# First FFN's output product as seven products of half size, with the last three modulation rows moved, in a hybrid layer on one core

## The chip, the core and the metric

The kernel runs on one core of a Trainium2 chip. The metric is device time in microseconds (us) of one execution, as the median of several runs. PE is TensorE, DVE is VectorE, ACT is ScalarE, POOL is GpSimd, SP is SyncE (here it only issues DMAs). Every engine works through its own list of instructions in the order written at build time.

## What is computed

```python
sh1, sc1, g1, sh2, sc2, g2, sh3, sc3, g3 = split(silu(c) @ w_ada + b_ada, 9)   # nine rows of 1024
u = rms_norm(x, ffn1_norm_g) * (1 + sc1) + sh1
x = x + 0.5 * g1 * swiglu(u, ffn1_w_in, ffn1_w_out)          # first FFN, d_ff = 2816
u = rms_norm(x, mix_norm_g) * (1 + sc2) + sh2
z = u @ w_mix + b_mix                                        # conv, mLSTM and forgetting attention
...                                                          # give y_a and y_b
merged = sigmoid(g_a) * (y_a @ w_branch_a) + sigmoid(g_b) * (y_b @ w_branch_b)
x = x + g2 * (merged @ w_out)
u = rms_norm(x, ffn2_norm_g) * (1 + sc3) + sh3
x = x + 0.5 * g3 * swiglu(u, ffn2_w_in, ffn2_w_out)          # second FFN
```

x is 512 tokens by 1024, all float32; swiglu(u) is (silu(a) * b) @ w_out with a, b the halves of u @ w_in.

## The kernel before

**Products.** A float32 product is made of three matmuls (mm3, L106 to L110): each operand is split in a high part (wh, uh, hh: ACT, L89 for weights) and a low part (wl, ul, hl: DVE, L91 for weights), and high x high, high x low and low x high are summed in PSUM. A weight tile arrives in `raw` (three buffers, 512 KB each, issued by SP at L79), is split into `wh` and `wl` (four buffers each), and is then free.

**Stages on PE, in order.** start (the first three blocks of the first FFN, while x is normed); first FFN-in (65 to 276 us); first FFN's output product (276 to 403); the mixer's products, mLSTM and attention; the branches (862 to 950) and w_out (to 1003); second FFN-in (1010 to 1241); second FFN's output product (from 1241).

**FFN-in.** 22 blocks j of 128 hidden columns. Each has two gemms, for a and b, of 8 k x 3 = 24 matmuls of 128x512 (gemm_stat). In the first FFN, ffn_h turns both into `hh` and `hl` (128x512 for each block).

**First FFN's output product, token_gemm.** Two halves of 512 output columns; in each, 22 k x 4 token blocks x 3 matmuls of 128x512, 264, thus 528 in all. A token block's result is scaled by the gate and added to x (DVE, `rs` and `x`, L575 and L577), squared and summed (ACT, L209). In the last token block of the second half norm_half(0) is woven in: from `ss` the mean `v`, a root in ten small DVE operations, `xn` (L236), 16 transposes on PE (L260), and then `uh`, `uf`, `ul` (u_from, L245 to L247) for the first 256 tokens of the mixer's input.

**Second FFN's output product, pair_out.** It is made by Strassen's scheme in Winograd's form: the product's three dimensions are cut in halves, and seven products of half size stand for eight: 11 pairs of blocks x 7 products x 2 x 3 = 462 matmuls of 128x512. pair_h makes, for each pair of blocks, sums of the four quarters of h (tiles `E`, `A1`, `Ra`, `Rb`, later `A2` by pair_split), and pair_weights makes sums of the quarters of w_out beside FFN-in: 22 units u, each of two loads `s` of 256 KB, four DVE sums of 128x256 (L434 to L437) and one store of 512 KB to `ws` in DRAM (L439). Z, Y, X and W are the four quarters of the result: Z and Y the first 256 tokens, W and X the last.

**Modulation rows.** ada_row makes one row v of 1024 from eight raw tiles of w_ada: DVE multiplies each by its column of c and accumulates (`acc`, L282 and L284); at the end the 128 partitions are folded (`fo`, L290), split in `hl` (L292), summed by two matmuls with a column of ones (`oneR`, L296), added to the bias `br` (L297) and stored (L298). Rows 0 and 1 are made in start, 2 to 6 beside first FFN-in, 7 and 8 beside token_gemm. mod_cols reads two rows back for a norm.

**What sets the order.** The program is written block by block; `extra` and `mid` are called between gemms and advance the generators ada_row and pair_weights by a step. The framework then orders each engine's list by its own estimates of when inputs are ready, under `issue_after` constraints, so an engine's list differs from the order of the code; it is fixed at build time. A `raw` tile waits for the third-last one to be split.

Of the kernel before, what the change touches and what calls it, by code (L numbers as in the profile page):

```python
# [46 lines left out]
class Layer:  # L47
    def __init__(self, tc, es, A, out, dbg=None):
# [223 lines left out]
    def ada_row(self, v, pool, bank):  # L272

        nc, A = self.nc, self.A
        acc = pool.tile([P, D], F32, name=self.nm("acc"), tag="xn", bufs=2)
        br = pool.tile([1, D], F32, name=self.nm("br"), tag="xn", bufs=2)
        for k in range(NK):
            r = self.raw([P, D], [(lambda t: t, A["w_ada"][0, k * P:(k + 1) * P, v * D:(v + 1) * D])])
            if k == 0:
                nc.sync.dma_start(br, A["b_ada"][:, v * D:(v + 1) * D])  # L280
                with self.tc.issue_after(self.last_ul.ins):
                    nc.vector.tensor_scalar(acc, r, self.ccol[:, 0:1], None, op0=MUL)  # L282
            else:
                nc.vector.scalar_tensor_tensor(acc, r, self.ccol[:, k:k + 1], acc, op0=MUL, op1=ADD)  # L284
            if k == NK - 1:
# [3 lines left out]
                nc.scalar.activation(t[0:64, :], acc[64:P, :], AF.Copy)  # L289
                nc.vector.tensor_tensor(acc[0:64, :], acc[0:64, :], t[0:64, :], op=ADD)  # L290
                nc.scalar.activation(hl[0:64, :], acc[0:64, :], AF.Copy)
                nc.vector.tensor_tensor(hl[64:P, :], acc[0:64, :], hl[0:64, :], op=SUB)  # L292
# [8 lines left out]
    def mod_cols(self, v, gain):  # L301
# [4 lines left out]
        b = self.tbank()  # L306
# [14 lines left out]
    def ffn_h(self, ps_a, ps_b, j, c0, c1, hp, tp):  # L321
        nc = self.nc
        w = c1 - c0
        s = self.tmp(tp, "sl")
        nc.scalar.activation(s[:, :w], ps_a[:, c0:c1], AF.Silu)
        nc.vector.tensor_tensor(s[:, :w], ps_b[:, c0:c1], s[:, :w], op=MUL)
        nc.scalar.activation(self.hh[j][:, c0:c1], s[:, :w], AF.Copy)
        nc.vector.tensor_tensor(self.hl[j][:, c0:c1], s[:, :w], self.hh[j][:, c0:c1], op=SUB)
# [780 lines left out]
    def run(self):  # L1109
# [205 lines left out]
```

## Time and profile before

| | us |
|---|---|
| median of 3 runs | 1354.39 (1353.95 to 1356.48) |
| the profiled execution | 1354.64 |
| its span | 1352.9 |
| first FFN-in | 65 to 276 |
| first FFN's output product | 276.1 to 402.7 |
| second FFN-in | 1010 to 1241 |
| second FFN's output product, matmuls | 1241.0 to 1345.9 |

The time of an execution is 1.74 us longer than the span, which runs from the first to the last instruction of the profile. A line of the profile names a line of the code, the engine, the operation and the tile that is written, then the tiles that are read. A matmul's own duration (389 ns for 128x512) is longer than the step from one matmul to the next, since they are pipelined; the step is what a matmul costs.

### The profile page before, as it was taken

What the parts mean: (1) busy time and instruction counts of PE and PEld (TensorE: products, weight loads), DVE (VectorE), ACT (ScalarE), POOL (GpSimd) and SP (SyncE); (2) the same over time, 40 slices, a digit from 0 to 9 for tenths busy, and PEclk for the clock granted to TensorE, in tenths of its full rate; (3) what the DMA queues carried; (4) which work ended last, traced back from release to release, by engine and by line L of the source; (5) the groups of instructions that cost most, each with busy time, mean ns of one, the idle gap of its engine ahead of it and who ended that gap; (6) DMA issues with size and microseconds to landing.
All of it is one profiled execution on the core that took longest, in us unless ns stands there. A gap on an engine that the chain in (4) does not pass through costs nothing.

```text
span 1352.9 us, 17800 instructions
## 1 busy us (share of the span) xinstructions
PE 1328.6 (98%) x6520; PEld 1113.0 (82%) x6520; DVE 887.8 (66%) x1661; ACT 589.4 (44%) x978; POOL 46.0 (3%) x71
## 2 busy tenths in 40 slices
PE   7999999999999999999999999999999999999997
PEld 6788887887888888988888888888788888888886
DVE  6866666655558767987686876446475655545776
ACT  4532333322235755556565676333353222223642
POOL 2000000000011101000000000002010000000000
PEclk9999999999999999999999999999999999999999
DMA  9676556665634434444243442354436677763474
GB/s 290 187 225 187 179 178 212 218 201 183 200 86 105 129 91 126 116 131 121 74 140 86 113 141 78 110 183 159 140 110 183 212 232 219 228 189 139 171 247 166
DMA packets 245691, 219.30 MB, mean 162 GB/s; under 512 B 12706, under 2 KB 206914, under 8 KB 245604
## 3 DMA queue, kind: packets, MB, share of 16 engines
q1 hardware_dynamic: 245124, 218.09, 52.9%
q8 instruction: 51, 0.84, 0.2%
q14 instruction: 36, 0.29, 0.1%
q0 software_dynamic: 416, 0.06, 0.0%
q10 hardware_dynamic: 64, 0.02, 0.0%
HBM read 194.47 MB, written 23.66 MB: 161 GB/s over the span
## 4 chain that ended last, share of the span: by engine, by line
PE 86%; DVE 7%; ACT 3%; DMA 2%; issue 1%; SPq 0%; DVEq 0%; ACTq 0%
PE g L110 22%; PE g L108 22%; PE g L109 22%; PE t L110 4%; PE t L108 4%; PE t L109 4%; PE g L697 2%; PE t L1041 2%; PE t L1011 1%; DVE wl L91 1%; PE t L982 1%; PE t L983 1%; PE t L697 1%; DVE fq L961 1%; DMA h_d<-hn 1%
## 5 line engine op out<-in xcount | busy, mean ns | idle before, releaser
L89 ACT ACTIVATE wh<-raw 128x1024 fp32r<-128x1024 f32 x236 | 244.2, 1040 | 434.1 <-PE g L109 143.4
L91 DVE TENSOR_TENSOR wl<-raw,wh 128x1024 fp32r<-128x1024 f32 x236 | 290.0, 1231 | 188.2 <-ACT wh L89 168.6
L108 PE MATMUL g<-uh,wh 128*128 128x512 f32 (+2 forms) x984 | 370.6, 377 | 0.8 <-ACT wh L89 0.7
L110 PE MATMUL g<-uh,wl 128*128 128x512 f32 (+2 forms) x984 | 369.6, 376 | 1.0 <-DVE wl L91 1.0
L109 PE MATMUL g<-ul,wh 128*128 128x512 f32 (+2 forms) x984 | 369.6, 376 | 0.0
L110 PEld LDWEIGHTS g<-uh,wl 128*128 128x128 f32 (+1 forms) x984 | 184.7, 188 | 35.7 <-DVE wl L91 1.8
L108 PEld LDWEIGHTS g<-uh,wh 128*128 128x128 f32 (+1 forms) x984 | 184.8, 188 | 34.5 <-ACT wh L89 1.4
L109 PEld LDWEIGHTS g<-ul,wh 128*128 128x128 f32 (+1 forms) x984 | 184.9, 188 | 33.2
L108 PE MATMUL g<-wh,uh 128*128 128x512 f32 (+1 forms) x320 | 111.9, 350 | 0.0
L110 PE MATMUL g<-wh,ul 128*128 128x512 f32 (+1 forms) x320 | 111.1, 347 | 0.0
L109 PE MATMUL g<-wl,uh 128*128 128x512 f32 (+1 forms) x320 | 110.9, 347 | 0.0
L284 DVE SCALAR_TENSOR_TENSOR acc<-raw,ccol,acc 128x1024 f32<-128x1024 f32 x49 | 62.8, 1282 | 13.0 <-DMA raw<-in_w_ada_dram 12.1
L108 PEld LDWEIGHTS g<-wh,uh 128*128 128x128 f32 x320 | 60.5, 189 | 7.8 <-DVE tk L896 0.5
L110 PEld LDWEIGHTS g<-wh,ul 128*128 128x128 f32 x320 | 60.5, 189 | 7.7
L109 PEld LDWEIGHTS g<-wl,uh 128*128 128x128 f32 x320 | 60.5, 189 | 7.4
L108 PE MATMUL g<-yh,wh 128*128 128x512 f32 x128 | 50.4, 394 | 0.0
L110 PE MATMUL g<-yh,wl 128*128 128x512 f32 x128 | 50.2, 392 | 0.0
L109 PE MATMUL g<-yl,wh 128*128 128x512 f32 x128 | 49.7, 388 | 0.0
L993 ACT ACTIVATE S<-S,mn 128x128 f32<-128x128 f32 (+1 forms) x64 | 35.6, 557 | 18.5 <-DVE mn L985 9.5
L108 PE MATMUL g<-wh,hh 128*128 128x512 f32 x88 | 35.0, 398 | 0.0
L110 PE MATMUL g<-wh,hl 128*128 128x512 f32 x88 | 34.9, 396 | 0.0
L108 PE MATMUL t<-wh,hh 128*128 128x512 f32 x88 | 34.8, 396 | 0.0
(319 smaller groups left out, 2054.8 us busy)
## 6 DMA issues: line engine op xcount, KB each, us to landing
raw<-in_ffn_w_in_dram SPq DMA_DIRECT2D x82, 512.0 KB
raw<-in_w_ada_dram SPq DMA_DIRECT2D x56, 512.0 KB
raw<-in_w_mix_dram SPq DMA_DIRECT2D x48, 512.0 KB
raw<-in_ffn_w_out_dram SPq DMA_DIRECT2D x33, 512.0 KB
s<-in_ffn_w_out_dram SPq DMA_DIRECT2D x44, 256.0 KB
ws<-s SPq DMA_DIRECT2D x22, 512.0 KB
ar<-in_w_ada_dram SPq DMA_DIRECT2D x32, 256.0 KB
raw<-in_w_mix_dram SPq DMA_DIRECT2D x32, 256.0 KB
```

Source lines behind the costliest of these rows:

```text
L89: nc.scalar.activation(hi, src, AF.Copy)
L91: nc.vector.tensor_tensor(lo, src, hi, op=SUB)
L108: mm(ps, lh, rh, start=start, stop=False)
L109: mm(ps, lh, rl, start=False, stop=False)
L110: self.last_mm = mm(ps, ll, rh, start=False, stop=stop)
L284: nc.vector.scalar_tensor_tensor(acc, r, self.ccol[:, k:k + 1], acc, op0=MUL, op1=ADD)
L697: mm = nc.tensor.matmul(acc_ps[b], (wl if p == 1 else wh)[:, b % 2, s], self.ul[k] if p == 2 else self.uh[k], start=k == 0 and p == 0, sto ...
L961: nc.vector.scalar_tensor_tensor(lo, b[own, :], gc[own, :], d[own, :], op0=MUL, op1=SUB)
L982: nc.tensor.matmul(ps[:, :w], q[:, s], k[:, :w], start=True, stop=False)
L983: nc.tensor.matmul(ps[:, :w], q[:, s], kl[:, :w], start=False, stop=True)
L993: nc.scalar.activation(S[:, ws], S[:, ws], AF.Exp, scale=-1.0, bias=m, accum_out=sm[:, qb:qb + 1])
L1041: nc.tensor.matmul(po[:, q0:], vt[:, kb, i, :], Px[:, o:o + T - q0], start=n == 1, stop=n == 8)
```

## The change

The first FFN's output product is made by pair_out too. So ffn_h gives way to pair_h, and pair_weights for ffn1_w_out runs beside first FFN-in, a step at each `mid` and `extra`. To make room, rows 2 to 5 are made there (before: 2 to 6), rows 6 and 7 beside the branches (one step for each of 16 branch products, with `acc` in two halves of 512), and row 8 beside second FFN-in. pair_out gets `last`: after Y it calls norm_half(0), and X and W are finished behind it, with squares in place of stores. The bias row `br` now takes a buffer of the `raw` ring, `acc` has one buffer, both `s` tiles lie in places of later `A` tiles, and the sum of the two branches is taken by DVE where POOL did it.

```diff
-    def ada_row(self, v, pool, bank):
+    def ada_row(self, v, new, bank):
...
             if k == NK - 1:
+                br = self.wp.tile([1, D], F32, name=self.nm("br"), tag="raw", bufs=3)
                 nc.sync.dma_start(br, A["b_ada"][:, v * D:(v + 1) * D])
...
-            self.ffn_act(pa, pb, j, 0, T, hp, tp)
+            self.pair_h(pa, pb, j, 0, T, hp, tp)
...
-            t = ts[u] = hp.tile([P, 5, 256], F32, name=self.nm("s"), tag=f"A{NP - 1}", bufs=1) if u % 2 else                 tp.tile([P, 5, 256], F32, name=self.nm("s"), tag="st", bufs=1)
+            t = ts[u] = hp.tile([P, 5, 256], F32, name=self.nm("s"), tag=f"A{NP - 2 + u % 2}", bufs=1)
...
-        def store(tb, half):
+            return t
+        def store(tb, half, t):
+            if last:
+                self.x_sq(tb, half, t)
+                return
...
+            if n == "Y" and last:
+                last()
...
-        self.ntmp, self.xn_tiles, self.ffn_act, self.gb_tag = 5, self.xn_start, self.ffn_h, ("gb", 1)
+        self.ntmp, self.xn_tiles, self.gb_tag = 4, self.xn_start, ("gb", 2)
...
-                ada = (s for v in (2, 3, 4, 5, 6) for s in self.ada_row(v, tp, self.gbank))
+                ada = (s for v in (2, 3, 4, 5) for s in self.ada_row(v, lambda: self.acc_ffn(tp), self.gbank))
+                pw = self.pair_weights(A["ffn1_w_out"][0], hp)
                 def extra(j):
-                    next(ada, None)
-                    next(ada, None)
-                    if j % 8 == 7:
+                    for _ in range(1 if j % 5 == 3 else 2):
                         next(ada, None)
-                self.ffn_in(A["ffn1_w_in"][0], NJ0, hp, tp, extra)
+                    next(pw, None)
+                self.ffn_in(A["ffn1_w_in"][0], NJ0, hp, tp, extra, lambda: next(pw, None))
...
-                    ada = self.ada_row(7 + half, tp, bank)
-                    extra = lambda: next(ada, None)
-                    self.token_gemm(lhs, NJ, A["ffn1_w_out"][0], half, self.residual(0.5, 2, half, tp), 2 + half, extra,
-                                    (lambda: self.norm_half(0, tp, G2, sh2)) if half else None)
...
+                self.pair_out(A["ffn1_w_out"][0], 2, hp, tp, lambda: self.x_load(A["x"][0]),
+                              lambda: self.norm_half(0, tp, G2, sh2))
             self.norm_half(1, tp, G2, sh2)
...
+            ada = (s for v in (6, 7) for s in self.ada_row(v, lambda: [self.tmp(bp, "acc") for _ in range(2)], self.tbank))
             for m in range(NK):
+                next(ada)
                 ta.append(self.branch(m, 0, bp, yp.tile([P, T], F32, name=self.nm("ta"), tag="qk", bufs=16), sg[m] if m < 2 else None))
             for m in range(NK):
                 t = self.branch(m, 1, bp, None)
-                nc.gpsimd.tensor_tensor(t, t, ta[m], op=ADD)
+                next(ada)
+                nc.vector.tensor_tensor(t, t, ta[m], op=ADD)
...
+            ada = self.ada_row(8, lambda: self.acc_ffn(tp), self.tbank)
...
+            def extra(j):
+                if j % 2:
+                    next(ada, None)
+                next(pw, None)
```

**The order at three places.** Where a row is folded beside first FFN-in, before, this is the DVE's list (row 3; `hl_266` is the folded row, `sl_252<-g_245` the activation of a block, which reads the end of its gemm):

```order
L284 SCALAR_TENSOR_TENSOR acc_228_1156<-raw_264_1381,ccol_155,acc_228_1156 128x1024
L290 TENSOR_TENSOR acc_228_1156<-acc_228_1156,fo_265_1384 64x1024
L292 TENSOR_TENSOR hl_266_1385<-acc_228_1156,hl_266_1385 64x1024
L326 TENSOR_TENSOR sl_252_1303<-g_245_1242,sl_252_1303 128x512
L91 TENSOR_TENSOR wl_276_1408<-raw_274_1405,wh_275_1407 128x1024
L328 TENSOR_TENSOR hl_153_753<-sl_252_1303,hh_131_731 128x512
L91 TENSOR_TENSOR wl_279_1438<-raw_277_1435,wh_278_1437 128x1024
L326 TENSOR_TENSOR sl_263_1376<-g_256_1315,sl_263_1376 128x512
L297 TENSOR_TENSOR br_229_1157<-g_267_1390,br_229_1157 1x512
L297 TENSOR_TENSOR br_229_1157<-g_268_1393,br_229_1157 1x512
```

and this the changed one's (row 3 again; `Ra_271<-g_262` is the product of a and b, which reads the end of gemm g_262; `s`, `E`, `Rb` and `A1` belong to the sums):

```order
L375 TENSOR_TENSOR Ra_271_1526<-g_262_1456,sl_270_1524 128x512
L434 TENSOR_TENSOR s_266_1491<-s_266_1491 128x256
L380 TENSOR_TENSOR E_257_1443<-E_257_1443,Ra_271_1526 128x256
L302 TENSOR_TENSOR hl_278_1545<-acc_217_1194,hl_278_1545 64x1024
L381 TENSOR_TENSOR E_257_1443<-E_257_1443 128x256
L435 TENSOR_TENSOR s_266_1491<-s_266_1491 128x256
L385 TENSOR_TENSOR Rb_272_1527<-Ra_271_1526,E_257_1443 128x256
L306 TENSOR_TENSOR br_276_1542<-g_279_1550,br_276_1542 1x512
L306 TENSOR_TENSOR br_276_1542<-g_280_1553,br_276_1542 1x512
L383 TENSOR_TENSOR A1_273_1529<-E_257_1443,A1_273_1529 128x768
L436 TENSOR_TENSOR s_266_1491<-s_266_1491 128x256
L91 TENSOR_TENSOR wl_285_1567<-raw_283_1564,wh_284_1566 128x1024
```

Before, fold and split (L290, L292) stand ahead of the product that reads a gemm, and two weight splits (L91) come between; in the change, hl and then wl_285 stand behind it. PE's list of the change at that place:

```order
L109 MATMUL g_262_1456<-ul_34_189,wh_268_1496 128x512
L110 MATMUL g_262_1456<-uh_26_181,wl_269_1497 128x512
L305 MATMUL g_279_1550<-hl_278_1545,oneR_128 1x512
L305 MATMUL g_280_1553<-hl_278_1545,oneR_128 1x512
L108 MATMUL g_281_1562<-uh_19_174,wh_284_1566 128x512
L109 MATMUL g_281_1562<-ul_27_182,wh_284_1566 128x512
L108 MATMUL g_282_1563<-uh_19_174,wh_288_1600 128x512
L109 MATMUL g_282_1563<-ul_27_182,wh_288_1600 128x512
L110 MATMUL g_281_1562<-uh_19_174,wl_285_1567 128x512
L108 MATMUL g_281_1562<-uh_20_175,wh_284_1566 128x512
L109 MATMUL g_281_1562<-ul_28_183,wh_284_1566 128x512
```

The two small matmuls (L305) stand right behind the gemm that Ra reads, and the next gemms' matmuls follow.

Later in that stage, around the weights of the 31st split of w_in, the DVE before (wl_364 is the 31st, g_346 the gemm of the 30th):

```order
L284 SCALAR_TENSOR_TENSOR acc_319_1705<-raw_355_1930,ccol_155,acc_319_1705 128x1024
L328 TENSOR_TENSOR hl_160_760<-sl_342_1849,hh_138_738 128x512
L290 TENSOR_TENSOR acc_319_1705<-acc_319_1705,fo_356_1933 64x1024
L91 TENSOR_TENSOR wl_364_1951<-raw_362_1948,wh_363_1950 128x1024
L292 TENSOR_TENSOR hl_357_1934<-acc_319_1705,hl_357_1934 64x1024
L91 TENSOR_TENSOR wl_367_1981<-raw_365_1978,wh_366_1980 128x1024
L326 TENSOR_TENSOR sl_353_1922<-g_346_1861,sl_353_1922 128x512
```

and in the change (wl_377 is the 31st, g_359 the gemm of the 30th):

```order
L375 TENSOR_TENSOR Ra_368_2075<-g_359_2005,sl_367_2073 128x512
L434 TENSOR_TENSOR s_363_2040<-s_363_2040 128x256
L380 TENSOR_TENSOR E_348_1976<-E_348_1976,Ra_368_2075 128x256
L435 TENSOR_TENSOR s_363_2040<-s_363_2040 128x256
L381 TENSOR_TENSOR E_348_1976<-E_348_1976 128x256
L436 TENSOR_TENSOR s_363_2040<-s_363_2040 128x256
L385 TENSOR_TENSOR Rb_369_2076<-Ra_368_2075,E_348_1976 128x256
L437 TENSOR_TENSOR s_363_2040<-s_363_2040 128x256
L91 TENSOR_TENSOR wl_377_2101<-raw_375_2098,wh_376_2100 128x1024
L383 TENSOR_TENSOR A1_370_2078<-E_348_1976,A1_370_2078 128x768
```

Before, the 31st and 32nd splits stand ahead of the product that reads the 30th gemm; in the change the 31st stands behind it and seven operations of 128x256.

Where the first FFN meets the mixer, the DVE before (`rs_522` and `x` are the third token block's end, then the norm; the last block's is `rs_523` and, for the other half's last, `rs_558`):

```order
L575 SCALAR_TENSOR_TENSOR rs_522_2999<-g_471_2658,gb_469_2655 128x512
L577 TENSOR_TENSOR x_4_137<-x_4_137,rs_522_2999 128x512
L230 SCALAR_TENSOR_TENSOR v_540_3041<-ss_410_2254,v_540_3041 128x2
...
L135 SCALAR_TENSOR_TENSOR rq_541_3044<-rt_542_3045,rq_541_3044 128x2
L236 TENSOR_SCALAR xn_544_3057<-x_1_134,rq_541_3044 128x512
L575 SCALAR_TENSOR_TENSOR rs_523_3021<-g_472_2659,gb_469_2655 128x512
L236 TENSOR_SCALAR xn_545_3060<-x_3_136,rq_541_3044 128x512
L577 TENSOR_TENSOR x_6_139<-x_6_139,rs_523_3021 128x512
L246 TENSOR_SCALAR uf_550_3083<-t_546_3063,G3_2652,sh3_2651 128x256
...
L247 TENSOR_TENSOR ul_538_3039<-uf_556_3107,uh_530_3031 128x256
L575 SCALAR_TENSOR_TENSOR rs_558_3133<-g_473_2660,gb_469_2655 128x512
```

and the change (`rs_634` is Y's last; `rs_669` the first of X, `x_587` at the end the last of W):

```order
L501 SCALAR_TENSOR_TENSOR rs_634_3298<-t_548_2873,gb_550_2876 128x512
L503 TENSOR_TENSOR x_582_3059<-x_582_3059,rs_633_3288 128x512
L503 TENSOR_TENSOR x_584_3061<-x_584_3061,rs_634_3298 128x512
L233 TENSOR_SCALAR v_651_3318<-ss_430_2430 128x2
L91 TENSOR_TENSOR wl_695_3539<-raw_693_3536,wh_694_3538 128x1024
L91 TENSOR_TENSOR wl_698_3545<-raw_696_3542,wh_697_3544 128x1024
L234 SCALAR_TENSOR_TENSOR v_651_3318<-ss_430_2430,v_651_3318 128x2
...
L91 TENSOR_TENSOR wl_701_3551<-raw_699_3548,wh_700_3550 128x1024
...
L251 TENSOR_TENSOR ul_649_3316<-uf_667_3384,uh_641_3308 128x256
L501 SCALAR_TENSOR_TENSOR rs_669_3398<-g_543_2868,gb_550_2876 128x512
L501 SCALAR_TENSOR_TENSOR rs_670_3402<-g_543_2868,gb_549_2874 128x512
...
L503 TENSOR_TENSOR x_587_3064<-x_587_3064,rs_674_3434 128x512
```

Three splits of the mixer's weights (wl_695, wl_698, wl_701) stand in the chain from rs_634 to xn, and the adds of X and W stand behind the first half's u (`ul_649` is its last). PE's list of the change there:

```order
L109 MATMUL g_542_2867<-wl_630_3259,A2_538_2859 128x512
L110 MATMUL g_542_2867<-wh_629_3258,Ra_539_2860 128x512
L264 MATMUL t_657_3340<-ident_103,xn_655_3334 128x128
L264 MATMUL t_658_3341<-ident_103,xn_655_3334 128x128
...
L264 MATMUL t_660_3343<-ident_103,xn_656_3337 128x128
L108 MATMUL g_705_3560<-uh_635_3302,wh_694_3538 128x256
L109 MATMUL g_705_3560<-ul_643_3310,wh_694_3538 128x256
...
L110 MATMUL g_707_3562<-uh_640_3307,wl_701_3551 128x256
L264 MATMUL t_681_3461<-ident_103,xn_679_3455 128x128
L264 MATMUL t_682_3462<-ident_103,xn_679_3455 128x128
...
L264 MATMUL t_684_3464<-ident_103,xn_680_3458 128x128
L108 MATMUL g_707_3562<-uh_641_3308,wh_700_3550 128x256
```

The transposes of the first half (xn_655) stand behind all of W's matmuls, those of the second (xn_679) behind 66 matmuls of 128x256.

More of the change, by code (lines that the diff above doesn't have):

```diff
@@ L299, in ada_row, with mod_cols @@
             yield
-    def mod_cols(self, v, gain):
+    def mod_cols(self, v, gain, bank):
         nc, sp, cp = self.nc, self.sp, self.cp
@@ L318, in mod_bcast @@
         return t
[L321 to L328, printed above, removed]
-    def h_tiles(self, hp):
-        self.hh = [hp.tile([P, T], F32R, name=self.nm("hh"), tag=f"hh{j}", bufs=1) for j in range(NJ)]
-        self.hl = [hp.tile([P, T], F32R, name=self.nm("hl"), tag=f"hl{j}", bufs=1) for j in range(NJ)]
     def ffn_in(self, w_in, j0, hp, tp, extra=None, mid=None):
@@ L445, in pair_weights, with pair_out @@
             yield
-    def pair_out(self, w, v, hp, tp, x_src):
+    def pair_out(self, w, v, hp, tp, x_src, last=None):
         nc = self.nc
@@ L497, in pair_out @@
         step = lambda n, tb, i, o: mm(banks[n], tb, *o[n], i == 0, i == NP - 1)
[L498 to L500 removed]
+        g = [self.mod_bcast(v, h, tp) for h in range(2)]
         def add(src, half, tbs):
```

100 lines of the change are left out of this document (48 added, 52 removed).

## The prediction

> **What bounds the kernel now.** I read the page first, then windows by stage, the matmuls by form, the waits of PE, the DVE's groups, and the timeline where the first FFN meets the mixer.
>
> ```profile
> PE 1328.6 (98%) x6520; PEld 1113.0 (82%) x6520; DVE 887.8 (66%) x1661; ACT 589.4 (44%) x978; POOL 46.0 (3%) x71
> PEclk9999999999999999999999999999999999999999
> DMA  9676556665634434444243442354436677763474
> ...
> 65.00:275.00 210.00, 208.75 (x920) 171.24 (x919) 135.79 (x138) 73.24 (x90) 0.00 (x0) 1.00 0.64 201
> 403.00:440.00 37.00, 36.60 (x257) 33.34 (x257) 32.49 (x62) 23.18 (x35) 7.47 (x15) 1.00 0.39 96
> 862.00:950.00 88.00, 88.00 (x386) 72.19 (x385) 45.60 (x46) 26.71 (x33) 10.12 (x7) 1.00 0.52 164
> 1010.00:1241.00 231.00, 231.00 (x1072) 193.49 (x1072) 122.66 (x215) 66.28 (x81) 3.42 (x4) 1.00 0.64 196
> 1241.00:1349.00 108.00, 104.91 (x463) 86.52 (x461) 82.32 (x106) 52.30 (x66) 0.00 (x0) 1.00 0.58 199
> ...
> 0.00:34.00 34.00, 23.86 (x143) 20.89 (x144) 23.03 (x68) 15.38 (x31) 9.51 (x22) 1.00 1.06 290
> ...
> PE t L178 <- DMA rowsC<-in_b_ada_dram: 5.6, 1, 5.6
> PE g L110 <- DVE wl L91: 1.0, 3, 0.5
> PE g L108 <- ACT wh L89: 0.7, 1, 0.7
> ```
>
> The columns of a window are its length, busy PE, PEld, DVE, ACT, POOL, then granted clock, DMA share and GB/s. PE is busy 98% of the span, at a full clock: every matmul taken away is time gained, and every wait put on PE is time lost. Other engines count only where they make PE wait. Today that is almost nowhere: 1.7 us for weights in the whole kernel.
>
> **What a matmul costs.** Start to start, first and last of a run of matmuls of 128x512:
>
> ```profile
> 199.66 0.39 PE L110 MATMUL g<-uh,wl 128*128 128x512 f32 x1
> 207.82 0.39 PE L110 MATMUL g<-uh,wl 128*128 128x512 f32 x1
> ...
> 393.81 0.40 PE L109 MATMUL g<-wl,hh 128*128 128x512 f32 x1
> 396.84 0.40 PE L110 MATMUL g<-wh,hl 128*128 128x512 f32 x1
> ...
> L109 PE MATMUL t<-wl,hh 128*128 128x512 f32 x88 | 34.8, 395 | 0.0
> L109 PE MATMUL t<-wl,A 128*128 128x512 f32 x88 | 34.2, 389 | 0.0
> ```
>
> In FFN-in 36 steps take 8.16 us, 0.2267 each; in the first FFN's output product 13 steps take 3.03, 0.2333 each. The second FFN's pair_out has the short form (389 ns beside 395). The slow tiles start at another place in the SBUF than the fast ones: hh starts 96 bytes past a multiple of 128, A in the second FFN 64. In the changed kernel the first FFN's A tiles start where hh did, so I take 0.2333. Both ends: 66 x 0.2333 = **15.4 us saved** (528 matmuls become 462); or, were the pitch 0.2267, 15.4 + 462 x 0.0066 = 18.5. The 16 transposes and the row's small matmuls move and stay in number. The Trainium skill ("TensorE: Matmul & The Clock Gate", section "Back-to-back issue gap") gives N/2.4 + 2.5, some 216 ns, for an isolated gap, by which the 66 would be 14.2; the trace's pitch is 5 to 8% above it and stands.
>
> **First FFN-in, where work is added.** Durations from the DVE's groups:
>
> ```profile
> L91 DVE TENSOR_TENSOR wl<-raw,wh 128x1024 fp32r<-128x1024 f32 x42 | 51.3, 1223 | 32.5 <-ACT wh L89 32.4
> L387 DVE TENSOR_TENSOR A<-E,A 128x768 fp32r<-128x768 f32 x10 | 9.5, 955 | 0.5 <-ACT A L386 0.5
> L437 DVE TENSOR_TENSOR s<-s 128x256 f32<-128x256 f32 x22 | 9.0, 423 | 0.3
> L373 DVE TENSOR_TENSOR E<-g,sl 128x512 f32<-128x512 f32 x10 | 6.9, 692 | 32.3 <-PE g L110 29.5 <-issue 2.8
> ...
> L284 DVE SCALAR_TENSOR_TENSOR acc<-raw,ccol,acc 128x1024 f32<-128x1024 f32 x35 | 44.9, 1282 | 2.5 <-DMA raw<-in_w_ada_dram 1.9
> L292 DVE TENSOR_TENSOR hl<-acc,hl 64x1024 fp32r<-64x1024 f32 x5 | 6.1, 1219 | 4.5 <-ACT hl L291 4.5
> L297 DVE TENSOR_TENSOR br<-g,br 1x512 f32<-1x512 f32 x8 | 5.1, 668 | 0.0
> ```
>
> DVE load: 135.8, less one row (7 x 1.28 + 0.75 + 2 x 1.22 + 2 x 0.67 = 13.5), plus 88 sums x 0.42 = 37, plus pair_h for the plain activation, about 4.0 us for two blocks where 2.7 were, 13 in all: 172 of 210 us. On average there is room; what costs is the order. At two places the DVE's next weights stand behind an instruction that must wait for the very gemm that PE is ending (the rows are with the change).
> - Row 3's fold. Ra waits for PE's last matmul, then come a sum, E, and hl; PE's next two matmuls need hl. A sum of 128x256 lasts 0.42 and lets the next one start after 0.34, a product of 128x512 after 0.6 (in the fence on the join below: 404.73 to 405.06, and on to 405.66). From the gemm's end: 0.69 + 0.34 + 0.34 + 1.22, less what overlaps at the start, 2.45 us with PE empty. Then E, s, Rb, the two br (they wait for those matmuls), A, s and wl stand ahead of PE's next product with wl. That is 0.34 x 4 + 0.67 x 2 + 0.95 + 1.2 = 4.9 us, of which 4 queued matmuls and the start cover 1.7: 3.2. Sum **5.7**.
> - Gemm 30. Ra again waits for the gemm's end, and seven operations of 128x256 stand before wl: 0.6 + 7 x 0.34 + 1.2 = 4.2 us against two matmuls (0.46) that PE has: **3.7**.
> - Row 4's fold, of the same kind, weaker: **1.0** (0 to 2).
>
> The same reading of before's order gives 1.3 us at one place, and the trace has 0.73 + 0.53 there (part of the 1.7 above). That stall isn't in the changed order: **-1.3**. Elsewhere in this stage, and in the second FFN, wl is written two gemms (10.9 us) ahead.
>
> **Transfers and queues.** Before, 42.2 MB take 0.64 of 210 us, 3.2 us a MB. After, 38 raw tiles and 32 of the rows at 0.52 MB, 44 s tiles at 0.26 and 22 stores at 0.52 are 59.7 MB: 190 us of the 221 that the stage then lasts. SP issues in order, and the s loads and stores wait on their own:
>
> ```profile
> SPq L439 <- DVE s L437: 45.1, 15, 6.3
> SPq L427 <- DMA ws<-s: 25.0, 18, 4.1
> ...
> SPq L298 <- DVE br L297: 16.6, 4, 5.5
> ```
>
> The first two rows are of the second FFN-in (us in total, times, longest), where the same steps made PE wait for nothing at a DMA share of 0.64; the third is the row's bias or store in the first. Here br also holds one of three raw slots until its store has landed. I take 0, since that nearest row shows 231.00 busy of 231; the other end is a rival below.
>
> **The join to the mixer.** Before, the last block's matmuls hide the first half's norm:
>
> ```profile
> 392.38 0.69 DVE L575 SCALAR_TENSOR_TENSOR rs<-g,gb 128x512 f32<-128x512 f32 x1 [2.78 <-PE g L110]
> 394.59 0.16 DVE L230 SCALAR_TENSOR_TENSOR v<-ss,v 128x2 f32<-128x2 f32 x1 [0.79 <-ACT rs L209]
> 396.77 0.49 DVE L236 TENSOR_SCALAR xn<-x,rq 128x512 f32<-128x512 f32 x1
> 400.10 1.00 DVE L246 TENSOR_SCALAR uf<-t,G,sh 128x256 f32<-128x256 f32 x2 [1.25 <-ACT uh L245]
> 404.73 0.42 DVE L247 TENSOR_TENSOR ul<-uf,uh 128x256 fp32r<-128x256 f32 x1
> 405.06 0.69 DVE L575 SCALAR_TENSOR_TENSOR rs<-g,gb 128x512 f32<-128x512 f32 x1
> 405.66 1.22 DVE L91 TENSOR_TENSOR wl<-raw,wh 128x1024 fp32r<-128x1024 f32 x1
> ...
> 397.32 0.66 PE L260 MATMUL t<-ident,xn 128*128 128x128 f32 x4
> 398.31 1.53 PE L260 MATMUL t<-ident,xn 128*128 128x128 f32 x12
> 402.70 0.28 PE L108 MATMUL g<-uh,wh 128*128 128x256 f32 x1
> 403.89 0.28 PE L109 MATMUL g<-ul,wh 128*128 128x256 f32 x1
> ```
>
> From rs to the first transpose 4.94 us; u takes 5.05 (400.10 to 405.15); a matmul of 128x256 takes 0.12 (10 steps, 1.19). In the changed order, from t = 0 at Y's last rs: three wl stand inside that chain (3 x 1.2, 0.5 of it in a wait that was idle), so the transposes start at 8.1, while X and W give PE 24 matmuls, until 5.4: idle **2.7**. Transposes until 10.1, then u until 15.1, with which PE's first product of 24 small matmuls keeps step: idle **3.0**. The DVE then does X's and W's twelve adds (12 x 0.6 = 7.2), squares, root and xn, 3.6: the second half's transposes stand at 25.9 in PE's queue, which has 42 small matmuls, until 20.8: idle **5.1**. Sum 10.8; before has 0.4 to 0.5 here: **+10.3**.
>
> **Branches and second FFN.** Rows 6 and 7: 32 half accumulations at 0.69, two folds and eight adds taken from POOL, about 30 us of DVE; 45.6 of 88 becomes 76, 16 more transfers make the DMA share 0.8. Row 8 adds 14 us of DVE and 12 of DMA to 122.7 and 148 of 231. Both hidden: idle DVE is the cover, and I found no wl behind a fold there. Bounds 0 to 2. No gain either: PE is full in both.
>
> **Sum.** -15.4 + 10.4 - 1.3 + 10.3 = +4.0 on a span of 1352.9. With 1.74 around it the profiled execution took 1354.64, 0.25 above the median 1354.39. So 1358.4 against that median, +0.3%. The measurement tells about 0.2%, 2.7 us, from no change: faster is below 1351.7, slower above 1357.1.
>
> **Rivals.**
> - The join is covered. If the DVE's chain finishes within X's and W's matmuls as before's did within its last block (for it: only 0.4 us of PE idle in 403:440; against it: the order, with three wl and twelve adds inside), its 10.3 isn't paid: 1348, or 1345 with the short pitch. It is faster once the join loses under 3.6.
> - First FFN-in bound by transfers. 59.7 MB need 206 us at 290 GB/s, the rate of the first 34 us, and SP's in-order waits keep it lower. At 270 it is 221, hidden by the stalls; at 250 it is 239, 18 more: 1376. For it: before's row accumulations already wait 1.9 us for raw. Against: the self-same steps cost nothing in the second FFN. Middle 1367.
> - The clock falls after a long wait. The start's wait of 5.6 us left it at 1.00 in 0:34. If the waits of 3.7 and 5.1 each halved the pitch's rate for as long again, half of that is lost: 4.4, so 1363. The Trainium skill says such ("TensorE: Matmul & The Clock Gate", section "Why this matters for your kernels": no idle of PE over about 3 us); the row speaks against it.
>
> **Numbers.** My reading 0.47 (1352 to 1363: same 0.15, slower 0.30, faster 0.02); covered join 0.25; transfers 0.23; clock 0.05. Faster 0.27, same 0.15, slower 0.58. Likeliest 1358.4. The range runs from the covered join with part of the short pitch, 1345, to three quarters of the transfers' price, 1372; outside lie 0.1 at either end.
>
> **What would show it.** The first FFN's output stage at some 108 us of matmuls, with pitch 0.2333 on A; PE waits of 2 to 4 us on hl and wl near the third row's fold and once later; waits at the transposes of both halves, 10 us in sum, and a clock at 1.00. PE waiting for ACT's wh or DVE's wl behind a late raw, with DMA near 1, is the second rival. Wrong it is if waits on PE sum to under 12 us or over 30.

## The result, and the profile after

The changed kernel takes 1387.11 us (median of 4 runs, 1384.58 to 1389.04) against 1354.83 (4 runs): ratio 1.0234, interval 1.0222 to 1.0247. It is slower by 32 us; 1358.4 was forecast, with 1345 to 1372 as the range. The profiled execution took 1387.51, its span 1385.7.

Stages by PE's timeline, from the first matmul of each to that of the next, in us:

| | before | changed | difference | forecast |
|---|---|---|---|---|
| until first FFN-in | 65.1 | 66.6 | +1.5 | 0 |
| first FFN-in | 211.0 | 241.8 | +30.8 | +9.1 |
| first FFN's output stage, first to last matmul | 126.4 | 108.3 | -18.1 | with the next row |
| to the mixer's first matmul | 0.2 | 14.1 | +13.9 | -5.1 for both |
| mixer, until the branches | 459.4 | 459.5 | +0.1 | in the row above |
| branches | 87.9 | 89.4 | +1.5 | 0 |
| w_out and the join behind it | 47.3 | 49.2 | +1.9 | 0 |
| second FFN-in | 243.7 | 244.6 | +0.9 | 0 |
| second FFN's output stage | 104.5 | 104.5 | 0 | 0 |

(The first row isn't of the change: in the profiled executions of the change and of f2_shift and join_pool (runs below) the clock was 0.50 for 3.4 us from 12 us on, and the row is 66.5 to 66.8; in the thirteen others, pad96, pad224 and zero_h with the change's start among them, it was not, and the row is 64.3 to 65.1.) The output stage did what was reckoned. First FFN-in did not. The page of the changed kernel (lines of it), and then three windows of it (first FFN-in, the output stage, the branches; columns as in the prediction):

```profile
PE 1328.8 (96%) x6454; PEld 1107.3 (80%) x6454; DVE 972.8 (70%) x1876; ACT 616.1 (44%) x1017; POOL 33.9 (2%) x63
PE   6998989899997999999999999999999999999997
DMA  9777978865673344354334253468535888774575
```

```profile
66.60:308.50 241.90, 220.03 (x923) 174.42 (x922) 161.91 (x245) 66.50 (x76) 0.00 (x0) 0.96 0.81 250
308.50:416.80 108.30, 108.08 (x463) 86.61 (x462) 79.62 (x103) 58.18 (x79) 0.13 (x1) 1.00 0.65 208
890.00:979.00 89.00, 88.87 (x388) 72.24 (x387) 62.61 (x87) 29.19 (x38) 0.00 (x0) 1.00 0.74 230
```

Before, PE was busy 209.75 of 211 us in first FFN-in (65.1 to 276.1, with 923 matmuls); now it is 220 of 242, with DMA at 0.81 (0.64) and a mean granted clock of 0.96. PE is not busy for 22 us, and the matmuls themselves, 923 again, take 10 us longer. PE's waits in the whole kernel, longest groups:

```profile
PE g L110 <- DVE wl L91: 8.2, 11, 2.0
PE g L108 <- ACT wh L89: 8.2, 4, 3.3
PE g L108 <- DVE rs L501: 6.0, 1, 6.0
PE g L305 <- DVE hl L302: 5.7, 3, 2.7
...
PE t L264 <- DVE xn L240: 4.7, 2, 4.2
...
PE t L108 <- DVE br L306: 1.6, 1, 1.6
```

wl and wh were 1.7 us before. The wait for rs is at the join to the mixer; that for br is at the start of w_out, whose first block needs the PSUM bank that row 7's fold still holds, and is the 1.9 of the table.

Where the clock was not granted, in windows around the waits:

```profile
131.40:138.20 6.80, 4.59 (x10) 3.19 (x11) 3.96 (x5) 2.31 (x4) 0.00 (x0) 0.50 0.55 166
138.20:168.90 30.70, 27.58 (x117) 21.55 (x117) 19.48 (x31) 6.43 (x8) 0.00 (x0) 1.00 0.93 282
168.90:172.30 3.40, 3.40 (x9) 2.63 (x8) 2.61 (x6) 1.06 (x1) 0.00 (x0) 0.50 0.95 275
```

Clock 0.50, for 6.8 and for 3.4 us, then 1.00 again. In 168.90:172.30 PE is busy throughout, with 9 matmuls where 15 fit at 0.2267. Counted over first FFN-in from start to start: 20 steps over 0.55 us (waits) take 26.3 us more than 0.2267 each, and 38 steps of 0.33 to 0.55, most of them 0.43, take 6.3 us more. Together 33.1 with rounding steps, against 2.0 before.

### The profile page after: what moved, and what is told of

The parts are those of the page before. It is cut to its first block, busy times and chain, and to the rows that moved or that the text cites. A ratio compares the mean times of both kernels' runs of the same rounds, so it can differ in the third digit from the quotient of the medians.

```text
span 1385.7 us, 18122 instructions
## 1 busy us (share of the span) xinstructions
PE 1328.8 (96%) x6454; PEld 1107.3 (80%) x6454; DVE 972.8 (70%) x1876; ACT 616.1 (44%) x1017; POOL 33.9 (2%) x63
## 4 chain that ended last, share of the span: by engine, by line
PE 69%; DMA 12%; DVE 11%; ACT 4%; issue 3%; SPq 1%; DVEq 0%; ACTq 0%
PE g L110 17%; PE g L108 17%; PE g L109 17%; DMA raw<-in_ffn_w_in_dram 6%; DVE wl L91 3%; PE t L108 3%; PE t L110 3%; PE t L109 3%; ACT wh L89 2%; DMA raw<-ws 2%; PE t L1038 1%; PE g L694 1%; PE t L1008 1%; PE t L979 1%; DMA raw<-in_w_branch_b_dram 1%
## 5 line engine op out<-in xcount | busy, mean ns | idle before, releaser
L89 ACT ACTIVATE wh<-raw 128x1024 fp32r<-128x1024 f32 (+1 forms) x258 | 262.5, 1022 | 460.1 <-DMA raw<-in_ffn_w_in_dram 139.2
L91 DVE TENSOR_TENSOR wl<-raw,wh 128x1024 fp32r<-128x1024 f32 (+1 forms) x258 | 302.7, 1176 | 169.6 <-ACT wh L89 166.8
L108 PE MATMUL g<-uh,wh 128*128 128x512 f32 (+2 forms) x984 | 375.1, 381 | 14.2 <-ACT wh L89 8.2
L110 PE MATMUL g<-uh,wl 128*128 128x512 f32 (+2 forms) x984 | 373.4, 380 | 8.2 <-DVE wl L91 8.2
L109 PE MATMUL g<-ul,wh 128*128 128x512 f32 (+2 forms) x984 | 372.9, 379 | 0.0
L108 PEld LDWEIGHTS g<-uh,wh 128*128 128x128 f32 (+1 forms) x984 | 187.4, 190 | 50.1 <-ACT wh L89 10.8
L110 PEld LDWEIGHTS g<-uh,wl 128*128 128x128 f32 (+1 forms) x984 | 186.9, 190 | 47.3 <-DVE wl L91 13.3
L109 PEld LDWEIGHTS g<-ul,wh 128*128 128x128 f32 (+1 forms) x984 | 187.5, 191 | 33.6
L108 PE MATMUL g<-wh,uh 128*128 128x512 f32 (+1 forms) x320 | 111.8, 350 | 0.0
L110 PE MATMUL g<-wh,ul 128*128 128x512 f32 (+1 forms) x320 | 111.1, 347 | 0.0
L109 PE MATMUL g<-wl,uh 128*128 128x512 f32 (+1 forms) x320 | 110.9, 347 | 0.0
L290 DVE SCALAR_TENSOR_TENSOR acc<-raw,ccol,acc 128x1024 f32<-128x1024 f32 (+1 forms) x63 | 65.1, 1045 | 45.7 <-DMA raw<-in_w_ada_dram 45.4
L108 PE MATMUL t<-wh,A 128*128 128x512 f32 x176 | 69.1, 393 | 0.0
L109 PE MATMUL t<-wl,A 128*128 128x512 f32 x176 | 69.0, 392 | 0.0
L108 PEld LDWEIGHTS g<-wh,uh 128*128 128x128 f32 x320 | 60.5, 189 | 7.9 <-DVE tk L893 0.5
L110 PEld LDWEIGHTS g<-wh,ul 128*128 128x128 f32 x320 | 60.5, 189 | 7.7
L109 PEld LDWEIGHTS g<-wl,uh 128*128 128x128 f32 x320 | 60.5, 189 | 7.3
L109 PE MATMUL g<-wl,A 128*128 128x512 f32 x132 | 51.8, 393 | 0.2 <-DVE wl L91 0.2
L108 PE MATMUL g<-wh,A 128*128 128x512 f32 x132 | 51.2, 393 | 0.0
L110 PE MATMUL g<-yh,wl 128*128 128x512 f32 x128 | 50.3, 393 | 0.0
L109 PE MATMUL g<-yl,wh 128*128 128x512 f32 x128 | 50.1, 391 | 0.1
L108 PE MATMUL g<-yh,wh 128*128 128x512 f32 x128 | 50.1, 391 | 0.0
```

What stands on the lines that cost most here:

```text
L89: nc.scalar.activation(hi, src, AF.Copy)
L91: nc.vector.tensor_tensor(lo, src, hi, op=SUB)
L108: mm(ps, lh, rh, start=start, stop=False)
L109: mm(ps, lh, rl, start=False, stop=False)
L110: self.last_mm = mm(ps, ll, rh, start=False, stop=stop)
L290: nc.vector.scalar_tensor_tensor(acc[h], r[:, sl[h]], c, acc[h], op0=MUL, op1=ADD)
```

## The experiments

**Two parts of the change taken alone.** SP's list around the second row's fold in the changed kernel:

```profile
110.99 0.31 SPq L294 DMA_DIRECT2D br<-in_b_ada_dram  x1
...
127.11 0.29 SPq L307 DMA_DIRECT2D mod_d<-br  x1
133.43 0.38 SPq L79 DMA_DIRECT2D raw<-in_ffn_w_in_dram  x1
```

and its wait, in SP's waits over the stage:

```profile
SPq L79 <- DMA mod_d<-br: 6.0, 1, 6.0
```

br takes a raw buffer at 111 and gives it back when its store has landed, 22 us later; a weight load waits 6.0 us for just that. PE lost 8.5 us in 122 to 138. First, br elsewhere:

```diff
-                br = self.wp.tile([1, D], F32, name=self.nm("br"), tag="raw", bufs=3)
+                br = [bp.tile([1, 512], F32, name=self.nm("br"), tag=tag, bufs=nb) for _ in range(2)]   # tag of gb
```

> The bias row br lies in the two gate buffers (gb) in place of one of the three raw buffers; nothing else is meant to change. In the changed kernel first FFN-in lasts 241.8 us (211.0 before); PE's waits and half-clock steps there add 33.1 us to the matmuls' own time, 25 of them in the four stretches in which a br held a raw buffer (111 to 133 us, 172 to 189, 231 to 252, 288 to 302). Theory R (the ring: with br in it two raw buffers are left for some 20 us in each fold, loads are issued late): first FFN-in falls by 12 to 18 us, the time to 1369 to 1375. Rival T (traffic: the loads and stores of the weight sums and SP's in-order waits make raw late, whoever holds a buffer): falls by under 4, the time stays above 1383.

1376.01 us, ratio 1.0154 (1.0139 to 1.0169): 11.1 less than the change. First FFN-in, the row below, falls by 11.6 to 230.2, just under the 12 to 18 of theory R. R holds for a third of the loss and no more: 21.4 us of waits and slow steps are left. (The branches took 93.7 us here, since br then shares the gates' two buffers there.)

```profile
64.60:294.80 230.20, 215.22 (x922) 173.35 (x920) 162.62 (x246) 66.41 (x78) 0.00 (x0) 0.97 0.86 264
```

Then the converse, this part alone in the kernel before (br's load too stands at the row's end there, as in the change):

```diff
-        br = pool.tile([1, D], F32, name=self.nm("br"), tag="xn", bufs=2)
...
+                br = self.wp.tile([1, D], F32, name=self.nm("br"), tag="raw", bufs=3)
```

> The kernel before with only this part of the change: br takes a raw buffer during the fold, in place of a place of its own. DMA share of first FFN-in stays 0.64. Theory R: the five folds beside first FFN-in (and two later) make PE wait, 5 to 15 us more than before, 1360 to 1370. Rival T: no more than 2 us, since the queue has room.

1362.39 us, ratio 1.0064 (1.0046 to 1.0081), within R's 1360 to 1370. First FFN-in 216.7 (211.0 before):

```profile
64.50:281.30 216.80, 212.66 (x924) 173.84 (x923) 134.76 (x137) 70.61 (x88) 0.00 (x0) 0.98 0.63 191
```

At a DMA share of 0.63 the lost buffer costs 6 us in five folds, beside the sums' load about twice that in four.

**The weight sums left out.**

```diff
-                pw = self.pair_weights(A["ffn1_w_out"][0], hp)
+                pw = iter(())          # ws then stands for rows of w_out
```

> The weight sums of the first FFN are left out (pair_weights does not run beside first FFN-in; pair_out reads rows of w_out where it read their sums, as many bytes), so 22 MB of transfers and 88 sums of 128x256 on DVE are gone from first FFN-in. Theory R (br in the raw ring): folds keep a raw buffer, waits stay: first FFN-in still above 224 us, time above 1368. Rival T (traffic): first FFN-in falls from 241.8 to 211 to 216 us, time 1356 to 1361.

1354.13 us in one run. First FFN-in:

```profile
65.00:278.60 213.60, 210.87 (x922) 172.86 (x920) 133.80 (x158) 67.43 (x79) 0.00 (x0) 0.99 0.61 181
```

213.6 us, although br still takes a raw buffer: T's 211 to 216 for the stage (the time is below T's 1356). So T holds as well, and R's number for this run was wrong: without the sums' load the stage is only 2.6 us longer than before. Neither is the cause by itself. Next, which half of the sums, both with br in the gate buffers:

```diff
             with self.tc.issue_after(self.last_mul.ins):
-                V(s(4), s(3), s(1), op=SUB)
...
```

> br_gb with the four DVE sums of each unit left out beside first FFN-in; the s loads and the ws stores stay (ws then holds rows of w_out, not their sums). br_gb: first FFN-in 230.2 us, of it 21.4 waits and half-clock steps. Theory B (bytes and their place in the queue make raw late): 224 us or more, time 1368 to 1377. Theory D (the sums stand ahead of weights in the DVE's list): 212 to 218, time 1357 to 1363.

```diff
-                    nc.sync.dma_start(t[:, 2 * n:2 * n + 2, :], w[r:r + P, :]...)
+            nc.gpsimd.memset(t, 0.0)
...
-            nc.sync.dma_start(self.ws[u // 2]..., ts.pop(u)[:, 1:5, :])
```

> The other half: br_gb with the DVE sums kept, on a tile that is set to zero once a unit (on POOL), and the s loads and ws stores left out; pair_out reads rows of w_out in place of the sums. Theory B: first FFN-in 212 to 218 us, time 1357 to 1363. Theory D: 224 or more, 1368 to 1377. If each half alone gives 212 to 220, neither is the cause by itself: they add up to more than the three raw buffers cover.

One run each, 1365.29 and 1355.08 us. Windows of first FFN-in, transfers alone and then DVE sums alone:

```profile
64.40:285.20 220.80, 212.21 (x923) 172.43 (x921) 134.89 (x159) 66.73 (x79) 0.00 (x0) 0.99 0.89 276
```

```profile
64.60:276.30 211.70, 209.85 (x923) 171.53 (x921) 159.89 (x245) 65.60 (x77) 23.79 (x20) 1.00 0.60 182
```

With the DVE's sums alone the stage lasts what it did before (211.7). The transfers alone cost 9 more (220.8, between the two expectations), and both together 18.6 (230.2). With the transfers a raw tile is late: from the issue of a w_in load until 95% of its packets have landed the median is 3.7 us before, 3.8 with DVE sums alone, 4.9 with transfers alone, 5.0 in br_gb and 4.5 in the change. That the DVE's longer list then has no slack to take the lateness is my reading of the three runs; none measures the slack.

**SP's list or the bytes?**

```diff
-                    nc.sync.dma_start(t[:, 2 * n:2 * n + 2, :], ...
+                    nc.gpsimd.dma_start(t[:, 2 * n:2 * n + 2, :], ...
...
-            nc.sync.dma_start(self.ws[u // 2]...
+            nc.gpsimd.dma_start(self.ws[u // 2]...
```

> As br_gb (br in the gate buffers; in the branches it stays in raw), and besides the loads and stores of the weight sums (s and ws) are issued by POOL, not by SP: as many bytes, but SP's list holds the raw loads alone, with no waits for sums or stores ahead of them. br_gb's first FFN-in lasts 230.2 us with 21.4 of PE's waits and half-clock steps; without the sums' transfers and DVE work 213.6 with 4.8. Theory Q (queue: raw loads stand behind waiting s and ws in SP's order): first FFN-in 212 to 219 us, time 1358 to 1366. Rival B (bytes: at 250 GB/s and more a load takes 6 us to land whoever issues it): stays above 225 us, time above 1370. Theory D (the DVE's sums stand ahead of the weights): the same as B.

1397.16 us, ratio 1.0314 (1.0280 to 1.0347): 10 slower than the change, and 21 slower than br_gb, which differs from it beside the FFNs by the issuer alone. First FFN-in takes 251.0 (230.2 in br_gb). Theory Q falls in the form stated. What POOL waited for in first FFN-in:

```profile
POOL s L434 <- DMA ws<-s: 90.9, 19, 8.1
POOL ws L446 <- DVE s L444: 90.0, 20, 22.3
```

and the DVE's timeline, where it waits for an s load that POOL had issued at 169.4:

```profile
177.14 0.42 DVE L441 TENSOR_TENSOR s<-s 128x256 f32<-128x256 f32 x1 [3.29 <-DMA s<-in_ffn_w_out_dram]
...
178.15 1.22 DVE L91 TENSOR_TENSOR wl<-raw,wh 128x1024 fp32r<-128x1024 f32 x1
```

The waits left SP's list and came back in the DVE's, with wl behind them. As issuing from POOL cost time in the second FFN-in too (249.9 in place of 244.6), this run doesn't tell what SP's order alone costs; that stays open.

**The folds' order, and the fourth row.** The row's two small matmuls are written one step later than its fold, so that hl stands ahead of Ra in the DVE's list; br as in br_gb beside the FFNs and in raw in the branches; the first FFN's tiles 224 bytes further on (below). First with row 5 moved to the branches, as a try at a better kernel:

```diff
+                if len(acc) == 1:
+                    yield                       # ahead of the two small matmuls
...
-                ada = (s for v in (2, 3, 4, 5) ...
+                ada = (s for v in (2, 3, 4) ...
...
-            ada = (s for v in (6, 7) ...
+            ada = (s for v in (5, 6, 7) ...
```

> A version from what the runs so far point to: br in the gate buffers beside the first FFN, row 5 moved to the branches (three rows beside first FFN-in, not four), the row's two small matmuls a step later than its fold, so that hl stands ahead of Ra in the DVE's list, and the 224 bytes of pad224. Against br_gb: row 5 and the folds took part in the 21.4 us of waits, so first FFN-in 216 to 223; output stage 104.5 to 108; join 13 to 14 as before. Time 1357 to 1366: faster than the change, not than the kernel before. If rows are not what crowds the stage: first FFN-in stays above 226, time above 1367.

1376.82 us, ratio 1.0152 (1.0128 to 1.0177). First FFN-in is as expected, 216.7, but the branches took 107 us: three rows there bring what the fourth brought here.

```profile
64.70:281.40 216.70, 211.46 (x921) 172.37 (x919) 150.37 (x235) 64.57 (x77) 0.00 (x0) 0.99 0.85 262
888.00:995.00 107.00, 95.46 (x365) 73.18 (x364) 73.83 (x103) 33.77 (x48) 0.00 (x0) 0.89 0.69 220
```

So the two edits apart: `mend` has row 5 back in its place, `mend2` has it in the first loop of pair_out.

```diff
+            if row:
+                next(row, None)                 # mend2 alone, in pair_out
```

> br in the gate buffers beside the FFNs, the row's two small matmuls a step after its fold, the 224 bytes; row 5 back beside first FFN-in and the branches with rows 6 and 7 as in the change. Theory O (the folds' place in the DVE's order): first FFN-in 216 to 221 us as in 'less' (216.7), against 230.2 in br_gb. Theory L (the fourth row's transfers beside the sums' load): 225 to 230. Output stage 106, join 13, branches 88 to 90. Time 1358 to 1363 by O, 1367 to 1373 by L.

> As 'mend', but row 5 is made in the first loop of the first FFN's pair_out (accumulated in two temporary tiles), so first FFN-in has three rows as in 'less' and the branches two as in the change. First FFN-in 215 to 218, output stage 106 to 109, join 13, branches 88 to 90: 1353 to 1359, that is within 0.3% of the kernel before on either side. If pair_out has no room for a row beside its own weights: output stage above 110, time above 1360.

`mend`: 1369.15 us, ratio 1.0105 (1.0089 to 1.0122); `mend2`: 1366.20, ratio 1.0079 (1.0054 to 1.0105). First FFN-in of `mend`, then of `mend2`:

```profile
65.10:290.20 225.10, 214.24 (x922) 170.21 (x920) 161.97 (x245) 66.05 (x76) 0.00 (x0) 1.00 0.87 271
```

```profile
65.00:282.40 217.40, 212.30 (x920) 173.14 (x918) 151.92 (x238) 64.30 (x76) 0.00 (x0) 0.98 0.84 259
```

The folds' order is worth 5.1 (230.2 to 225.1), row 5 (its transfers, DVE work and fold) another 7.7 (to 217.4). Both sizes hold the rows' pace too, which differs: a row takes two steps at every call of `extra` in `mend`, one or two in the others. `mend` lies where theory L put it. `mend2` loses 6 us of that again in the output stage (111.8 in place of 105.8), as its expectation allowed. No version here beats the kernel before.

**The join.**

```diff
+                G = nc.gpsimd.tensor_tensor if last and n in "XW" else V     # X's and W's adds to x
```

> The changed kernel, with X's and W's six adds to x at the end of the first FFN taken by POOL; the six scalings stay on DVE. In the changed kernel 14.1 us pass from the last matmul of the first FFN to the mixer's first, 2 of them transposes; PE waits 4.3 for xn and then 6.0 for a scaling (rs), since the mixer's first products need the PSUM banks of X and W. If the DVE's list of adds sets that second wait: 6 x 0.6 = 3.6 us shorter, join 10 to 11.5 us, time 1382 to 1385. If u sets it: no change of the join, 1386 to 1388; if the second half's transposes now wait for POOL, what is won is lost again behind the first 66 small products.

1393.78 us, ratio 1.0298 (1.0281 to 1.0315). The join is 12.6 us (14.1 in the change), which tells nothing: in pad96, zero_h, f2_shift and pad224 below, with the change's join, it is 12.2 to 14.2, and PE's wait for rs is 6.0 here too. So the adds don't set that wait. POOL's six adds run until 435.8 and the second half's transposes wait; the first 1000 matmuls behind the join take 185.6 in place of 178.9:

```profile
428.35 7.48 POOL L503 TENSOR_TENSOR x<-x,rs 128x512 f32<-128x512 f32 x6
```

PE's waits for xn, 4.7 us in the change, are here:

```profile
PE t L264 <- DVE xn L240: 8.2, 3, 4.4
```

This loss behind the adds was written as the third outcome.

**What sets the pitch of 0.2333.** Three runs with the first or second FFN's tiles elsewhere, and one with other values:

```diff
+                pad = pd.tile([P, 24], F32, name="pad")      # pad96; 56 in pad224; 776 ahead of the second FFN in f2_shift
```

> The changed kernel with an unused tile of 96 bytes ahead of the first FFN's A tiles, so that these start 64 bytes past a multiple of 128 as those of the second FFN do (they started 96 past it); the orders on PE, ACT and SP are unchanged, DVE has one small memset more. If the place of the stationary operand sets the pitch (0.2333 against 0.2267): 462 x 0.0066 = 3.0 us less, time 1383 to 1385, pitch in the first FFN's output stage 0.2267. If it does not: 1386 to 1388, pitch 0.2333.

> The changed kernel with the second FFN's tiles moved up by 3104 bytes, to the very addresses that the first FFN's have; orders unchanged but for a small memset. In the first FFN's output stage a matmul of 128x512 takes 0.2333 to 0.2340, in the second's 0.2267, and 32 times another place mod 128 (pad96) did not alter that. If the place in the SBUF sets it in any way: 0.2333 in the second too, 3 us more. If it is the data or the stage: 0.2267 stays.

> The first FFN's activation is multiplied by zero (so its output product adds nothing to x); all instructions and their order stay. If the values in the stationary operand set the pitch of the first FFN's output stage, it falls from 0.2333 to 0.2267 or less there, 3 us or more; if not, it stays 0.2333. First FFN-in and the join stay as they are: 1384 to 1388 otherwise.

> The changed kernel with 224 unused bytes ahead of the first FFN's A tiles: they then start 192 bytes past a multiple of 256, as the second FFN's (0.2267) and the weight buffers do. Starts seen so far with 0.2331 to 0.2340: 224 (the change), 64 (pad96) and, for w_out's mh, 0 past a multiple of 256; and the second FFN at the first's addresses (f2_shift) had 0.2331 too. If the place mod 256 counts: 0.2267 and 3 us less in the first FFN's output stage. If not: 0.2331 as before.

One group of matmuls of the output stage (mean ns of one behind the busy us), first in the change:

```profile
L109 PE MATMUL t<-wl,A 128*128 128x512 f32 x88 | 34.7, 395 | 0.0
```

in pad224:

```profile
L109 PE MATMUL t<-wl,A 128*128 128x512 f32 x88 | 34.4, 391 | 0.3 <-DVE wl L91 0.3
```

and in the second FFN of f2_shift, where it was 389 before:

```profile
L109 PE MATMUL t<-wl,A 128*128 128x512 f32 x86 | 33.9, 395 | 0.0
```

pad96 has 395 and zero_h 397. From start to start: 0.2331 in the change and zero_h, 0.2325 in pad96; 0.2273 in pad224; and 0.2331 in the second FFN of f2_shift, which has 0.2267 elsewhere. So it is the place in the SBUF and not the values. Slow are starts 0 (w_out, 0.2332), 64 and 224 bytes past a multiple of 256, fast is 192. A rule mod 256 fits these; four places don't prove it. Nor is the stationary operand's place all: the branches' products, whose weights lie in the same ring of buffers as first FFN-in's, take 0.229 (0.2317, 0.2257 and 0.2294 for L108, L109 and L110) against 0.2267 there. Which of the other operands does that was not tested. pad96 took 1384.33 us (ratio 1.0217, 1.0202 to 1.0233), inside what its expectation gave for success, yet its pitch hardly changed (0.4 us over the stage): the 2.8 us lie elsewhere, by the profiles 2.2 ahead of first FFN-in, where the change's had the clock at 0.50, and 1.9 at the join. pad224 took 1387.98 (1.0238, 1.0222 to 1.0254): its output stage is 2.2 us shorter and first FFN-in 2.5 longer than the change's. f2_shift and zero_h took 1387.36 and 1389.41, one run each. Here the stage's rows decide and the total doesn't.

## Why the prediction was wrong

- **The step that failed: "I take 0" for transfers and queues in first FFN-in.** It was taken from the nearest row, the second FFN-in, where the same sums made PE wait for nothing. That stage had a DMA share of 0.64 and no rows; this one has 0.81 (the working's own 190 of 221 us is 0.86), four rows and a raw ring that a fold cuts to two. In place of 0 the stage lost 30.8 us, 21.7 more than the forecast 9.1 of the order's stalls; part of it is the clock's (below). By taking parts away: br 11.6; then the folds' order 5.1 and row 5 7.7, or else the sums' transfers 18.6 or their DVE work 9.4. These overlap: br without the sums cost 2.6 and 5.7, the DVE's sums without transfers 0.6. So the runs show that the load is the cause, and no one share of it.
- **The rival was right in kind, and at its dear end nearly in size.** It gave 239 us for the stage at 250 GB/s; measured are 241.8 at 250. I gave it 0.23 and cut the range at three quarters of its price. Yet the pipe wasn't full: `mend` moves the same bytes at 271 GB/s in 225 us. Loads were issued late because buffers came free late, and each took about 1 us longer to land (4.5 against 3.7); such lateness adds to the stalls of the order, where I had let those hide it.
- **The order's stalls came where they were read.** Row 3's fold: forecast 5.7, measured 6.3 with slow steps. Row 4's: 1.0, measured 2.3. Gemm 30: 3.7, measured 5.8 with slow steps, and both causes stand there at once:

```profile
254.32 2.67 DVE L290 SCALAR_TENSOR_TENSOR acc<-raw,ccol,acc 128x1024 f32<-128x1024 f32 x2 [2.70 <-DMA raw<-in_w_ada_dram]
...
257.07 0.69 DVE L375 TENSOR_TENSOR Ra<-g,sl 128x512 f32<-128x512 f32 x1
...
260.27 1.23 DVE L91 TENSOR_TENSOR wl<-raw,wh 128x1024 fp32r<-128x1024 f32 x1 [0.16 <-ACT wh L89]
```

```profile
260.29 0.50 PE L108 MATMUL g<-uh,wh 128*128 128x512 f32 x1 [3.33 <-ACT wh L89]
...
261.55 0.79 PE L110 MATMUL g<-uh,wl 128*128 128x512 f32 x1 [0.53 <-DVE wl L91]
```

  Ra to wl takes 3.2 us, as reckoned; PE's own wait is put down to wh, whose raw was late. Of the other 18 us none was forecast: 9.0 in 110 to 139 (row 2's fold, where the working saw no stall and br's store held up a weight load), 5.8 in 152 to 173 (wh and wl behind late raw tiles), the rest in single waits.
- **The clock rival (0.05) came true, and the row against it was misread.** I argued from a clock of 1.00 in 0:34, behind a wait of 5.6 us. But the record of the clock in that trace begins at 9.3 us. Until then, right behind the wait, PE's transposes start 0.213 us apart, and from then on 0.109, like later ones. Here all 24 of them, and 16 later ones, before:

```profile
5.77 4.55 PE L670 MATMUL t<-ident 128*128 128x128 f32 x24
...
412.36 1.95 PE L260 MATMUL t<-ident,xn 128*128 128x128 f32 x16
```

  So that row didn't speak against the rival. In the changed kernel the clock fell to 0.50 for 3.4 or 6.8 us at a time: behind steps (from one matmul's start to the next) of 3.18 and 2.61, of 2.18 with 0.92 soon after, of 3.09 and 3.72, and at the join. The length of one wait doesn't decide it: steps of 3.41 in dma_only and 3.08 in br_gb left the clock as it was, while 2.23 and 1.56 close together in br_gb halved it. The clock changes only on a grid of 3.41 us. Count each step of PE as work up to 0.2333 us, and take the pieces of that grid at a clock of 1.00 in all 16 traces: where work filled less than 0.40 of a piece, the next one had 0.50, in 59 of 59; between 0.40 and 0.47 in 4 of 16; above that in none of 6041. So waits in one piece add up, and one wait may fall into two pieces and cost no clock. Its price here is 6.3 us in first FFN-in, near the 4.4 of the rival. The Trainium skill ("TensorE: Matmul & The Clock Gate", section "Why this matters for your kernels") states a rule of this kind, no idle of PE over about 3 us. The trace agrees in kind, but not on the length of a single wait: 2.18 with 0.92 sufficed, 3.41 once did not.
- **Matmuls right, the join right in its sum.** 18.1 us of the output stage less the 2.0 of transposes and 0.9 of the row's matmuls that moved away are 15.2, for 15.4 forecast. The join, on PE and then on the DVE:

```profile
416.78 0.40 PE L110 MATMUL g<-wh,Ra 128*128 128x512 f32 x1
421.34 3.55 PE L264 MATMUL t<-ident,xn 128*128 128x128 f32 x16 [4.16 <-DVE xn L240]
430.86 0.55 PE L108 MATMUL g<-uh,wh 128*128 128x256 f32 x1 [5.97 <-DVE rs L501]
```

```profile
414.25 2.36 DVE L91 TENSOR_TENSOR wl<-raw,wh 128x1024 fp32r<-128x1024 f32 x2
...
419.47 1.22 DVE L91 TENSOR_TENSOR wl<-raw,wh 128x1024 fp32r<-128x1024 f32 x1
...
429.10 0.42 DVE L251 TENSOR_TENSOR ul<-uf,uh 128x256 fp32r<-128x256 f32 x1
429.43 1.28 DVE L501 SCALAR_TENSOR_TENSOR rs<-g,gb 128x512 f32<-128x512 f32 x2
```

  The splits of wl stand in the chain as read, and PE waits 4.16 + 5.97 = 10.1 for 10.8 forecast (2.7, 3.0 and 5.1). But PE can't keep step with u: the mixer's first product needs a PSUM bank that X's scaling frees, and that stands behind all of u. So PE starts later and the second half's transposes wait only 0.5 us for their xn (4.7 in all). Size right, place half wrong: that 4.2 and 6.0 make up for the missing 5.1 is luck.
- **Branches and w_out: +1.5 and +1.9 for 0 to 2**, the latter a PSUM bank, which the working didn't look at.

## What to carry to other kernels

Work that is hidden in one stage is not free in the next: take its price from a row with the same sum of loads (transfers, ring buffers, the helping engine's list), and add a lateness of buffers to the stalls that the order forces. A small tile that borrows a slot of a load ring counts for as long as it is held, here 22 us of a three-deep ring, not by its size. Add up PE's waits that stand close together: where they left less than 0.40 of a 3.41 us piece to matmuls, the next 3.41 us went at half the clock.

## What the runs showed of the hardware

- A matmul of 128x512 in pair_out costs 0.2267 to 0.2273 us from start to start with its stationary tiles 192 bytes past a multiple of 256, and 0.2325 to 0.2331 with them at 64 or 224 (pad96, pad224, f2_shift): 3.0 us over 462 in f2_shift. The branches' 0.229 shows that other places or operands matter too.
- PE's clock is granted in pieces of 3.41 us. It was halved behind every piece (59 of 59) of which matmuls filled under 0.40, and behind none (of 6041) filled above 0.47; matmuls of 128x512 then take 0.43 us from start to start.
- Small adds of 128x512 on POOL ran at 1.25 us each (7.48 for 6 in join_pool), twice the DVE's 0.6 (3.9 for 6 in the change).
